# Transposes and gate products of a background chain recorded as one run on TensorE

## The chip, the cores and the metric

The kernel runs on one core of one Trainium2 chip. The metric is device time in microseconds (us) of one launch; lower is better. Engines are named as the profile names them: PE is TensorE (PEld its weight loads), DVE is VectorE, ACT is ScalarE, POOL is GpSimd, SP issues the DMAs of the weight stream. PSUM is the memory into which PE writes; SBUF is the working memory that the other engines read and write.

## What is computed

A decoder block for 256 tokens of width 2048, in float32. Cut to what matters:

```python
xn = rms_norm(x)
proj = xn @ w_in                       # 2048 x 26720, split in three
y_ssm = ssd_branch(p_ssm) @ w_branch_ssm   # 8 groups, causal conv, gated, scanned in chunks of 128
y_gdn = gdn_branch(p_gdn) @ w_branch_gdn   # 16 heads, causal conv, triangular inverse, gated
h = x + (gates[0] * y_ssm + gates[1] * y_gdn) @ w_out
hn = rms_norm(h)
q = hn @ w_q                           # 8 heads x 2 x 128
s = q . sub_keys                       # two lists of 128 scores per head, top 16 of each,
                                       # top 16 of the 256 sums: 128 experts of 16384 per token
out = rms_norm(h + sum over chosen experts of gate * gelu(u[e] . hn) * v[e])
```

The kernel does the last line densely: it multiplies hn with the whole table u (16384 x 2048), multiplies the activations with a gate that is zero for every expert that wasn't chosen, and multiplies the result with the whole table v.

## The kernel before

**The stream.** All large matrices (w_in, the two branch matrices, w_out, w_q, u, v) pass through one stream of 512 KB units of 128 x 1024 floats. SP loads a unit into one of four `raw` buffers. `Stream.split` (line 100) cuts it into a high part `whi` (ACT, line 107) and a low part `wlo` (DVE, line 108), which go into one of three cut buffers; `Stream.next` (line 113) hands a cut unit to PE and splits up to two units ahead. `product` (line 373) makes three products of each piece (lines 384 to 386: high by high, high by low, low by high) of 512 columns for both halves of the tokens: 12 products of 512 columns to a unit. PE takes its instructions strictly in order.

**Background chains.** Everything else is written as Python generators: `gdn_gen` and `ssm_gen` for the two mixers, `mt_gen` and `h_gen` for transposes of activations, `score_gen` for the keys, `gate_gen` for the dense gate, `act_gen` for the activations of each piece of u. After each piece of a unit, `product` calls `bg.step()`: it runs up to two chains that are due, each up to its next `yield`. Whether a chain is due is decided while the program is recorded, from a table of estimated durations (class `Clock`): a chain's next step is due once what it recorded last is estimated to be through. So a `yield` costs a chain at least a wait until its last result is through, and the position of each instruction in an engine's order is fixed when the program is built. `bg.drain(es)` runs chains until the named ones are finished, with no product of the stream in between.

**What a step holds.** A step that transposes takes one PSUM tile (`ps_tile()`, name `pst`, four buffers), records four transposes of 128x128 (`tr`, line 316) into it, records the evacuation on ACT or DVE, and yields; the next step does the other half. `score_gen` makes its scores (line 1056) in the same way.

**The dense gate.** `gate_gen` (line 1083) comes after the four score chains. For every four tokens, `build(n)` (line 1124) makes two one-hot tiles on DVE (`oa`, line 1130; `ob`, line 1131, a single buffer) and multiplies `ob` by the gates on POOL (`b2`, line 1132). Eight f16 products of 128x128 (line 1149) turn them into a PSUM tile, ACT copies that into `stages` (line 1151), and after each second build 512 KB are written to the DRAM tile `gdr` (line 1153). There are 64 builds; build n+2 is recorded in the step that multiplies build n.

**Where it is needed.** The table u is done in 32 pieces (`for u in range(32)`, line 1199), with one `act_gen` for each, which writes 512 KB to `hdr`. Before piece 31 the kernel drains `gate_gen`, then ACT issues two loads of 1 MB from `gdr` (`gate_load`, line 1184) and two of 512 KB from `hdr` (`coef_load`, line 1188). The first coefficients (`coef`, lines 1194 to 1197) are made at k == 13 of piece 31. Then comes the stage of table v (lines 1222 to 1228).

Of the kernel before, what the change touches and what calls it, by code (L numbers as in the profile page):

```python
# [240 lines left out]
def block(ctx, tc, nc, I, out, dbg=None):  # L241
# [488 lines left out]
    def ssm_gen(g, pt, bce, zg, yref):  # L730
# [25 lines left out]
        y = mx.tile([128, 2, 512], F, name="ys", bufs=1)  # L756
        for tb in range(2):
            p = ps_tile()
            for c in range(4):
                tr(p[:, c * 128:(c + 1) * 128], xT[:, c, tb * 128:(tb + 1) * 128])  # L760
            p3 = p.rearrange("p (h d) -> p h d", h=8)
# [53 lines left out]
        for c2 in range(2):  # L815
            p = ps_tile().rearrange("p (a b) -> p a b", a=2)
            for a in range(2):
                c = 2 * c2 + a
                for tb in range(2):
                    tr(p[:, a, tb * 128:(tb + 1) * 128], y[:, tb, c * 128:(c + 1) * 128])  # L820
            for a in range(2):
                c = 2 * c2 + a
                split_t(yh[:, c, :], yl[:, c, :], p[:, a, :], snw[:, 4 * g + c:4 * g + c + 1])
            yield
# [53 lines left out]
    def mt_gen(n):  # L878
        if n == 3:
            yield  # L880
        for k2 in (2 * n, 2 * n + 1):
            p = ps_tile().rearrange("p (a b) -> p a b", a=2)
            for a in range(2):
                for tb in range(2):
                    tr(p[:, a, tb * 128:(tb + 1) * 128], accs[0][:, tb, (2 * k2 + a) * 128:(2 * k2 + a + 1) * 128])
            split_t(mh[:, 2 * k2:2 * k2 + 2, :], ml[:, 2 * k2:2 * k2 + 2, :], p, 0.5)
            yield
# [107 lines left out]
    def h_gen(n):  # L995
        for c2 in range(2):
            p = ps_tile().rearrange("p (a b) -> p a b", a=2)
            for a in range(2):
                k = 4 * n + 2 * c2 + a
                for tb in range(2):  # L1000
                    tr(p[:, a, tb * 128:(tb + 1) * 128], h[:, tb, k * 128:(k + 1) * 128])
# [41 lines left out]
    def score_gen(i, q):  # L1043
        qT = pp.tile([128, 4, T], F, name="p4", bufs=6)
        for c2 in range(2):
            p = ps_tile().rearrange("p (a b) -> p a b", a=2)
            for a in range(2):
                for tb in range(2):
                    tr(p[:, a, tb * 128:(tb + 1) * 128], q[:, tb, (2 * c2 + a) * 128:(2 * c2 + a + 1) * 128])
            S.activation(qT[:, 2 * c2:2 * c2 + 2, :], p, AF.Copy)  # L1050
            yield
        sc = pp.tile([128, 2, 4, 128], F, name="p4", bufs=6)
        for tb in range(2):
            p = ps_tile().rearrange("p (a b) -> p a b", a=4)
            for a in range(4):
                PE.matmul(p[:, a, :], qT[:, a, tb * 128:(tb + 1) * 128], keys[:, 4 * i + a, :], start=True, stop=True)
# [26 lines left out]
    def gate_gen(score_es):  # L1083
# [53 lines left out]
        nxt = [build(0)]  # L1137
        yield
        nxt.append(build(1))
        for n in range(64):  # L1140
            yield
            oa, b2 = nxt.pop(0)
            if n < 62:
                nxt.append(build(n + 2))
            stage = stages[:, (n // 2) % 4]
            p = ps_tile().rearrange("p (a b) -> p a b", a=4)
# [214 lines left out]
```

## Time and profile before

| | |
|---|---|
| median of 3 runs | 3410.59 us (3410.57 to 3413.02) |
| the profiled execution's own time | 3411.41 us |
| span of the profiled execution | 3409.6 us |
| PE busy | 3374.3 us, 99% of the span |
| DVE, ACT, POOL busy | 2248.6, 1732.8, 533.6 us |
| mean granted clock of PE | 0.997 |
| piece 31 of u begins on PE | 2668.61 us |
| last gate product begins | about 2570.4 us |

A timeline row has the start in us, the duration in us, engine, line, operation, the tiles written and read, the shapes, the number of merged instructions, and in brackets the idle time of the engine just before with what ended it. A duration of PE holds the pipeline's fill, so the distance from one start to the next is what an instruction costs there. "ACTq" is ACT's queue issuing a DMA.

### The profile page before, as it was taken

How to read it: one execution, taken by the hardware profiler on the slowest of the kernel's cores; microseconds unless marked ns; L12 is line 12 of the kernel's file. 1: busy time of each engine (PE TensorE's matmuls, PEld its weight loads, DVE VectorE, ACT ScalarE, POOL GpSimd, SP SyncE). 2: the span in 40 equal slices, each digit the busy share in tenths (PEclk: the TensorE clock that was granted, in tenths of full speed). 3: DMA queues.
4: the chain of work that ended last, by engine and by line, in shares of the span. 5: the costliest groups of instructions: out<-in, count | busy, mean ns of one | idle time of the engine just before them, and what ended most of it. 6: DMA issues, size and time to landing. Idle time of an engine off the chain costs nothing.

```text
span 3409.6 us, 43675 instructions
## 1 busy us (share of the span) xinstructions
PE 3374.3 (99%) x15958; PEld 2773.3 (81%) x15958; DVE 2248.6 (66%) x3214; ACT 1732.8 (51%) x2308; POOL 533.6 (16%) x835
## 2 busy tenths in 40 slices
PE   9999999999999999999999999999999999999998
PEld 7888887878888888888788888888888788888886
DVE  6666776766677777777665888766664455555555
ACT  6555555554445454544444544556565444444444
POOL 0435253545001000000000000133320000000000
PEclk9999999999999999999999999999999999999999
DMA  7655564555555555555566566677776877777765
GB/s 263 194 162 172 162 187 152 181 161 179 180 187 182 183 182 185 185 174 193 186 218 186 172 212 213 212 232 233 234 232 219 266 242 242 243 237 242 243 231 161
DMA packets 254776, 692.33 MB, mean 203 GB/s; under 512 B 31248, under 2 KB 92000, under 8 KB 254304
## 3 DMA queue, kind: packets, MB, share of 16 engines
q1 hardware_dynamic: 164960, 594.03, 54.3%
q10 hardware_dynamic: 84000, 87.60, 7.8%
q0 software_dynamic: 5600, 7.91, 0.8%
q8 instruction: 125, 2.05, 0.2%
q14 instruction: 91, 0.75, 0.1%
HBM read 650.13 MB, written 39.41 MB: 202 GB/s over the span
## 4 chain that ended last, share of the span: by engine, by line
PE 95%; DVE 3%; ACT 1%; issue 1%; ACTq 0%; DMA 0%; POOL 0%; POOLq 0%; DVEq 0%; SPq 0%
PE acc L384 22%; PE acc L385 22%; PE acc L386 22%; PE acc L1223 3%; PE acc L1222 3%; PE acc L1228 3%; PE pst L1222 3%; PE pst L1223 3%; PE pst L1228 3%; PE pst L316 3%; DVE wlo L108 1%; PE pst L1149 1%; PE pst L781 1%; DVE t L459 1%; ACT whi L107 0%
## 5 line engine op out<-in xcount | busy, mean ns | idle before, releaser
L108 DVE TENSOR_TENSOR wlo<-raw,whi 128x1024 fp32r<-128x1024 f32 (+1 forms) x1129 | 1415.2, 1261 | 895.8 <-ACT whi L107 894.6
L107 ACT ACTIVATE whi<-raw 128x1024 fp32r<-128x1024 f32 (+1 forms) x1129 | 1184.0, 1053 | 945.3 <-PE acc L386 531.4
L384 PE MATMUL acc<-whi,t 128*128 128x512 f32 (+2 forms) x2848 | 1150.9, 404 | 8.7 <-ACT whi L107 8.7
L385 PE MATMUL acc<-wlo,t 128*128 128x512 f32 (+2 forms) x2848 | 1109.8, 390 | 6.2 <-DVE wlo L108 6.0
L386 PE MATMUL acc<-whi,t 128*128 128x512 f32 (+2 forms) x2848 | 1109.2, 389 | 0.0
L385 PEld LDWEIGHTS acc<-wlo,t 128*128 128x128 f32 x2848 | 537.5, 189 | 115.0 <-DVE wlo L108 12.3
L384 PEld LDWEIGHTS acc<-whi,t 128*128 128x128 f32 x2848 | 537.0, 189 | 113.5 <-ACT whi L107 8.9
L386 PEld LDWEIGHTS acc<-whi,t 128*128 128x128 f32 x2848 | 536.4, 188 | 113.7
L1132 POOL TENSOR_TENSOR b<-ob,gp 128x1024 f16<-128x1024 f16 x64 | 121.5, 1898 | 608.0 <-DVE ob L1131 608.0
L384 PE MATMUL acc<-whi,yh 128*128 128x512 f32 x512 | 207.8, 406 | 0.0
L385 PE MATMUL acc<-wlo,yh 128*128 128x512 f32 x512 | 200.1, 391 | 1.6 <-DVE wlo L108 1.6
L1223 PE MATMUL pst<-wlo,t 128*128 128x512 f32 x512 | 199.3, 389 | 2.1 <-DVE wlo L108 2.1
L386 PE MATMUL acc<-whi,yl 128*128 128x512 f32 x512 | 199.9, 390 | 0.0
L1222 PE MATMUL pst<-whi,t 128*128 128x512 f32 x512 | 199.4, 389 | 0.0
L1222 PE MATMUL acc<-whi,t 128*128 128x512 f32 x512 | 199.2, 389 | 0.0
L1223 PE MATMUL acc<-wlo,t 128*128 128x512 f32 x512 | 199.2, 389 | 0.0
L1228 PE MATMUL pst<-whi,t 128*128 128x512 f32 x508 | 156.4, 389 | 0.0
L1228 PE MATMUL acc<-whi,t 128*128 128x512 f32 x508 | 156.4, 389 | 0.0
L459 DVE SCALAR_TENSOR_TENSOR t<-pst,cols,t 128x255 f32<-128x255 f32 x336 | 135.8, 472 | 20.6 <-ACT t L455 20.5
L1151 ACT ACTIVATE t<-pst 128x512 f32<-128x512 f32 x64 | 76.8, 1199 | 80.9 <-PE pst L1149 80.9
L385 PEld LDWEIGHTS acc<-wlo,yh 128*128 128x128 f32 x512 | 96.3, 188 | 23.3 <-DVE wlo L108 2.9
L1223 PEld LDWEIGHTS pst<-wlo,t 128*128 128x128 f32 x512 | 96.1, 188 | 22.3 <-DVE wlo L108 2.4
(294 smaller groups left out, 3279.4 us busy)
## 6 DMA issues: line engine op xcount, KB each, us to landing
raw<-w_in SPq DMA_DIRECT2D x408, 512.0 KB
raw<-u SPq DMA_DIRECT2D x256, 512.0 KB
raw<-v SPq DMA_DIRECT2D x256, 512.0 KB
raw<-w_gdn SPq DMA_DIRECT2D x64, 512.0 KB
raw<-w_ssm SPq DMA_DIRECT2D x64, 512.0 KB
raw<-w_out SPq DMA_DIRECT2D x32, 512.0 KB
raw<-w_q SPq DMA_DIRECT2D x32, 512.0 KB
hdr<-ht ACTq DMA_DIRECT2D x32, 512.0 KB
```

The lines of the kernel that those rows point to most:

```text
L107: self.nc.scalar.activation(hi[:, s], t[:, s], AF.Copy)
L108: self.nc.vector.tensor_tensor(lo[:, s], t[:, s], hi[:, s].bitcast(F), op=OP.subtract)
L316: PE.transpose(dst, src, ident)
L384: PE.matmul(o, xa, h_, start=k == 0, stop=False)
L385: PE.matmul(o, xa, l_, start=False, stop=False)
L386: PE.matmul(o, xb, h_, start=False, stop=k == nk - 1)
L459: V.scalar_tensor_tensor(dst[:, s:], src[:, :T - s], w[:, c, k:k + 1], dst[:, s:], op0=OP.mult, op1=OP.add)
L1132: G.tensor_tensor(b2, ob[:, None, :, :].to_broadcast([128, 2, 4, 128]), gp[:, :, ts, None].to_broadcast([128, 2, 4, 128]), op=OP.mult)
L1151: S.activation(stage[:, :, q:q + 4].rearrange("p i t -> p t i"), p, AF.Copy, scale=1.0 / GSCALE)
L1222: PE.matmul(o_, a, hi[:, s], start=i2 == 0, stop=False)
L1223: PE.matmul(o_, a, lo[:, s], start=False, stop=False)
L1228: PE.matmul(acc[tb][2 * hv + n], b, hi[:, n * 512:(n + 1) * 512], start=False, stop=False)
```

## The change

At each of these places a chain now takes two PSUM tiles at once, records all its transposes (or products) into both in one go, and then evacuates the two tiles in two steps as before: `conv_silu`, `ssm_gen` (two places), `mt_gen`, `h_gen`, `score_gen` (two places), `gate_gen`, `act_gen`. In `conv_silu` the input tile is also released (`unread.pop(0)`) after the transposes. `gate_gen` is rewritten: four builds are made ahead, one to a step; then for each of 32 pairs of builds a step records 16 products into two tiles, both evacuations and the write to `gdr`, and the next two builds follow in steps of their own. `oa` and `b2` get four buffers instead of three; `ob` keeps one.

```diff
     def conv_silu(pool, src, nch, chunk_of, w, bias, dst):
         y = pool.tile([128, 4, T], F, name="t4", bufs=NT4[0])
+        ps = []
         for i0 in range(0, nch, 2):
             p = ps_tile().rearrange("p (a b) -> p a b", a=2)
             for a in range(2):
                 for tb in range(2):
                     tr(p[:, a, tb * 128:(tb + 1) * 128], src(tb, i0 + a))
+            ps.append(p)
+        unread.pop(0)
+        for i0, p in zip(range(0, nch, 2), ps):
             conv([(y[:, i0 + a, :], p[:, a, :], chunk_of(i0 + a)) for a in range(2)], w, bias)
             yield
-        unread.pop(0)
...
         def build(n):
             ts = slice(4 * n, 4 * n + 4)
-            oa = pp.tile([128, 4, 128], F16, name="oa", bufs=3)
+            oa = pp.tile([128, 4, 128], F16, name="oa", bufs=4)
             ob = pp.tile([128, 4, 128], F16, name="ob", bufs=1)
-            b2 = pp.tile([128, 2, 4, 128], F16, name="b2", bufs=3)
+            b2 = pp.tile([128, 2, 4, 128], F16, name="b2", bufs=4)
...
-        nxt = [build(0)]
-        yield
-        nxt.append(build(1))
-        for n in range(64):
+        nxt = []
+        for n in range(4):
+            nxt.append(build(n))
             yield
-            oa, b2 = nxt.pop(0)
-            if n < 62:
-                nxt.append(build(n + 2))
-            stage = stages[:, (n // 2) % 4]
-            p = ps_tile().rearrange("p (a b) -> p a b", a=4)
-            for t in range(4):
-                for s in range(2):
-                    PE.matmul(p[:, t, :], oa[:, t, :], b2[:, s, t, :], start=s == 0, stop=s == 1)
-            q = (n % 2) * 4
-            S.activation(stage[:, :, q:q + 4].rearrange("p i t -> p t i"), p, AF.Copy, scale=1.0 / GSCALE)
-            if n % 2:
-                S.dma_start(gdr[n // 2], stage)
+        for m in range(32):
+            stage = stages[:, m % 4]
+            pair = [nxt.pop(0), nxt.pop(0)]
+            ps = [ps_tile().rearrange("p (a b) -> p a b", a=4) for _ in range(2)]
+            for (oa, b2), p in zip(pair, ps):
+                for t in range(4):
+                    for s in range(2):
+                        PE.matmul(p[:, t, :], oa[:, t, :], b2[:, s, t, :], start=s == 0, stop=s == 1)
+            for q, p in enumerate(ps):
+                S.activation(stage[:, :, 4 * q:4 * q + 4].rearrange("p i t -> p t i"), p, AF.Copy, scale=1.0 / GSCALE)
+            S.dma_start(gdr[m], stage)
+            for n in (2 * m + 4, 2 * m + 5):
+                if n < 64:
+                    yield
+                    nxt.append(build(n))
+            yield
...
     def act_gen(u, ps):
...
-        for c2 in range(2):
-            p = ps_tile().rearrange("p (a b) -> p a b", a=2)
-            for a in range(2):
-                for tb in range(2):
-                    tr(p[:, a, tb * 128:(tb + 1) * 128], a_[:, tb, (2 * c2 + a) * 128:(2 * c2 + a + 1) * 128])
+        ps = [ps_tile().rearrange("p (a b) -> p a b", a=2) for _ in range(2)]
+        for a in range(4):
+            for tb in range(2):
+                tr(ps[a // 2][:, a % 2, tb * 128:(tb + 1) * 128], a_[:, tb, a * 128:(a + 1) * 128])
+        for c2, p in enumerate(ps):
             S.activation(ht[:, 2 * c2:2 * c2 + 2, :], p, AF.Copy)
             yield
```

The other places (`ssm_gen`, `mt_gen`, `h_gen`, `score_gen`) are written like `act_gen`. In the changed kernel the lines of the build are 1132 (`oa`), 1133 (`ob`) and 1134 (`b2`), the gate products 1150, their evacuation 1152, `gate_load` 1189, `coef_load` 1193, the Gelu of `act_gen` 1173 and its evacuation 1181.

**PE, one piece of table u (`act_gen`).** p is the activation tile, cst the identity. Before, the eight transposes stand as two fours around two pieces of a unit:

```order
L386 MATMUL acc<-whi,t_15362 128x512
L316 MATMUL pst<-cst,p_23268 128x128 x4
L384 MATMUL acc<-whi,t_15361 128x512
L385 MATMUL acc<-wlo,t_15361 128x512
L386 MATMUL acc<-whi,t_15362 128x512
L384 MATMUL acc<-whi,t_15361 128x512
L385 MATMUL acc<-wlo,t_15361 128x512
L386 MATMUL acc<-whi,t_15362 128x512
L316 MATMUL pst<-cst,p_23268 128x128 x4
L384 MATMUL acc<-whi,t_15361 128x512
```

After, at the same place in another piece:

```order
L385 MATMUL acc<-wlo,t_15361 128x512
L386 MATMUL acc<-whi,t_15362 128x512
L316 MATMUL pst<-cst,p_21970 128x128 x8
L384 MATMUL acc<-whi,t_15361 128x512
L385 MATMUL acc<-wlo,t_15361 128x512
```

The second four moved up behind the first. Over the whole program the runs of background work between two products of the stream go from 418 to 320; the gate products go from 64 runs of eight (16 of them with four transposes in the same run) to 24 runs of sixteen and one last run.

**DVE, the end of `gate_gen`.** Before, with the last two builds (oa and ob) between splits of units, and 44 splits after them until the first coefficient (L1194):

```order
L1130 TENSOR_TENSOR oa<-iob,i1T 128x512
L1131 TENSOR_TENSOR ob<-iob,i2T 128x512
L108 TENSOR_TENSOR wlo<-raw,whi 128x1024 x2
L1130 TENSOR_TENSOR oa<-iob,i1T 128x512
L1131 TENSOR_TENSOR ob<-iob,i2T 128x512
L108 TENSOR_TENSOR wlo<-raw,whi 128x1024 x44
L1194 TENSOR_TENSOR p_23440<-p_23440,m_23436 128x1024
L1197 TENSOR_TENSOR t_23435<-p_23440,t_23435 128x1024
```

After, from the splits of the first two units of piece 31 on:

```order
L108 TENSOR_TENSOR wlo_23144<-raw_23047,whi_23143 128x1024
L108 TENSOR_TENSOR wlo_23162<-raw_23066,whi_23161 128x1024
L1132 TENSOR_TENSOR oa_23184<-iob_16075,i1T_16077 128x512
L1133 TENSOR_TENSOR ob_23185<-iob_16075,i2T_16078 128x512
L1132 TENSOR_TENSOR oa_23203<-iob_16075,i1T_16077 128x512
L1133 TENSOR_TENSOR ob_23204<-iob_16075,i2T_16078 128x512
L1132 TENSOR_TENSOR oa_23230<-iob_16075,i1T_16077 128x512
L1133 TENSOR_TENSOR ob_23231<-iob_16075,i2T_16078 128x512
```

and the last two of these builds, up to the split of the third unit of piece 31:

```order
L1132 TENSOR_TENSOR oa_23395<-iob_16075,i1T_16077 128x512
L1133 TENSOR_TENSOR ob_23396<-iob_16075,i2T_16078 128x512
L1132 TENSOR_TENSOR oa_23401<-iob_16075,i1T_16077 128x512
L1133 TENSOR_TENSOR ob_23402<-iob_16075,i2T_16078 128x512
L108 TENSOR_TENSOR wlo_23460<-raw_23090,whi_23459 128x1024
```

The last 14 builds (50 to 63) have moved into the drain ahead of piece 31, with no split between them. On PE the products of builds 48 to 63 and the eight transposes of piece 30 stand there too, behind the last product of piece 30 and ahead of the first of piece 31.

**ACT, the same place.** Before:

```order
L107 ACTIVATE whi<-raw 128x1024 x6
L1168 ACTIVATE p_23431<-acc,r_16065 128x512 x2
L1184 DMA m_23436<-gdr 128x16x128 x2
L1188 DMA p_23440<-hdr 128x1024
L1188 DMA p_23442<-hdr 128x1024
L107 ACTIVATE whi<-raw 128x1024
```

After, from the last but one write of `gdr` on:

```order
L1153 DMA gdr<-t_19054 128x1024
L1152 ACTIVATE t_19054<-pst 128x4x128 x2
L1153 DMA gdr<-t_19054 128x1024
L1189 DMA m_23449<-gdr 128x16x128 x2
L1193 DMA p_23453<-hdr 128x1024
L1193 DMA p_23455<-hdr 128x1024
L107 ACTIVATE whi<-raw 128x1024 x7
```

The loads from `gdr` now stand directly behind the last write to it; the second of them reads what that write wrote and waits for it. The `whi` behind them is the third unit of piece 31.

## Rows read from the trace of the kernel before

**Rows 1.** The page: busy time of PE with its share of the span and instructions, and the granted clock of PE in 40 slices of the span, in tenths.

```profile
PE 3374.3 (99%) x15958; PEld 2773.3 (81%) x15958; DVE 2248.6 (66%) x3214; ACT 1732.8 (51%) x2308; POOL 533.6 (16%) x835
...
PEclk9999999999999999999999999999999999999999
```

**Rows 2.** What PE waited for over the whole span: us in total, times, longest.

```profile
PE acc L384 <- ACT whi L107: 8.7, 2, 6.3
PE acc L385 <- DVE wlo L108: 7.6, 14, 0.8
...
PE pst L655 <- ACT mm L651: 1.8, 2, 1.6
```

**Rows 3.** Timeline of PE around four runs of background work: eight gate products; eight gate products and four transposes; four transposes; eight transposes.

```profile
2570.18 0.40 PE L386 MATMUL acc<-whi,t 128*128 128x512 f32 x1
2570.42 0.62 PE L1149 MATMUL pst<-b,oa 128*128 128x128 f16 x8
...
2571.16 0.40 PE L385 MATMUL acc<-wlo,t 128*128 128x512 f32 x1
...
2555.40 0.39 PE L386 MATMUL acc<-whi,t 128*128 128x512 f32 x1
2555.63 0.62 PE L1149 MATMUL pst<-b,oa 128*128 128x128 f16 x8
2556.09 0.61 PE L316 MATMUL pst<-cst,p 128*128 128x128 f32 x4
...
2556.76 0.39 PE L385 MATMUL acc<-wlo,t 128*128 128x512 f32 x1
...
2602.94 0.39 PE L386 MATMUL acc<-whi,t 128*128 128x512 f32 x1
2603.17 0.60 PE L316 MATMUL pst<-cst,p 128*128 128x128 f32 x4
...
2603.84 0.39 PE L385 MATMUL acc<-wlo,t 128*128 128x512 f32 x1
...
1720.51 0.39 PE L386 MATMUL acc<-whi,t 128*128 128x512 f32 x1
1720.74 1.03 PE L316 MATMUL pst<-cst,t 128*128 128x128 f32 x8
...
1721.85 0.40 PE L385 MATMUL acc<-wlo,t 128*128 128x512 f32 x1
```

**Rows 4.** The line of the build on POOL over all its instructions: number, duration in ns (least, median, most), first and last start.

```profile
L1132 POOL TENSOR_TENSOR b<-ob,gp x64: 1896/1897/1900, 2172.7 to 2563.6; 128x1024 f16<-128x1024 f16 x64
```

**Rows 5.** Timeline of DVE and of POOL around the last build.

```profile
2562.19 0.68 DVE L1130 TENSOR_TENSOR oa<-iob,i1T 128x512 f16<-128x512 f16 x1
2562.79 0.69 DVE L1131 TENSOR_TENSOR ob<-iob,i2T 128x512 f16<-128x512 f16 x1
2564.58 2.03 DVE L108 TENSOR_TENSOR wlo<-raw,whi 128x1024 fp32r<-128x1024 f32 x1 [1.10 <-ACT whi L107]
...
2563.62 1.90 POOL L1132 TENSOR_TENSOR b<-ob,gp 128x1024 f16<-128x1024 f16 x1 [4.38 <-DVE ob L1131]
```

**Rows 6.** Timeline of POOL and of DVE where POOL's instruction came second (at 1277), and where it ran alone (at 1257).

```profile
1257.78 1.29 POOL L799 TENSOR_TENSOR ys<-ys,zg 128x512 f32<-128x512 f32 x1 [18.87 <-DVE ys L783]
1277.07 2.21 POOL L799 TENSOR_TENSOR ys<-ys,zg 128x512 f32<-128x512 f32 x1 [18.01 <-DVE ys L793]
...
1276.91 1.22 DVE L108 TENSOR_TENSOR wlo<-raw,whi 128x1024 fp32r<-128x1024 f32 x1
```

**Rows 7.** Timeline of POOL and of DVE at the end of the span, where DVE waits for a result of POOL.

```profile
3402.69 0.55 POOL L313 TENSOR_TENSOR r<-m,half 128x1 f32<-128x1 f32 x1 [3.65 <-DVE m L1242]
...
3403.28 1.28 DVE L1248 SCALAR_TENSOR_TENSOR t<-t,r,t 128x1024 f32<-128x1024 f32 x1 [0.67 <-POOL r L313]
```

**Rows 8.** Timeline of PE, DVE and ACT at the start of piece 31.

```profile
2668.61 0.39 PE L384 MATMUL acc<-whi,t 128*128 128x512 f32 x1
...
2671.33 0.60 PE L316 MATMUL pst<-cst,p 128*128 128x128 f32 x4
...
2677.53 0.79 PE L384 MATMUL acc<-whi,t 128*128 128x512 f32 x1 [2.39 <-ACT whi L107]
...
2667.18 1.23 DVE L108 TENSOR_TENSOR wlo<-raw,whi 128x1024 fp32r<-128x1024 f32 x1 [1.50 <-ACT whi L107]
...
2668.81 3.25 ACTq L1184 DMA_DIRECT2D m<-gdr  x2
2672.09 4.23 ACTq L1188 DMA_DIRECT2D p<-hdr  x2
2676.43 1.06 ACT L107 ACTIVATE whi<-raw 128x1024 fp32r<-128x1024 f32 x1 [6.93 <-DMA m<-gdr]
```

**Rows 9.** Timeline of ACT behind the last but one gate product, and the DMA queues from 2572.3 to 2576.1 us (packets, MB, share of 16 engines); q10 is ACT's.

```profile
2571.10 1.20 ACT L1151 ACTIVATE t<-pst 128x512 f32<-128x512 f32 x1
2572.32 0.33 ACTq L1153 DMA_DIRECT2D gdr<-t  x1
...
q10 hardware_dynamic: 144, 0.52, 49.8%
```

**Rows 10.** Two stretches at the start of piece 31: length, busy time and number of instructions on PE, PEld, DVE, ACT and POOL, granted clock of PE, share and rate of the DMA engines.

```profile
2677.50:2684.00 6.50, 6.00 (x13) 4.42 (x14) 3.67 (x3) 2.95 (x5) 0.00 (x0) 0.50 1.05 390
2684.00:2690.00 6.00, 6.00 (x28) 4.90 (x26) 2.45 (x2) 2.49 (x3) 0.00 (x0) 0.99 0.64 230
```

More of the change, by code (lines that the diff above doesn't have):

```diff
@@ L756, in ssm_gen @@
         y = mx.tile([128, 2, 512], F, name="ys", bufs=1)
+        ps = [ps_tile() for _ in range(2)]
         for tb in range(2):
-            p = ps_tile()
             for c in range(4):
-                tr(p[:, c * 128:(c + 1) * 128], xT[:, c, tb * 128:(tb + 1) * 128])
-            p3 = p.rearrange("p (h d) -> p h d", h=8)
+                tr(ps[tb][:, c * 128:(c + 1) * 128], xT[:, c, tb * 128:(tb + 1) * 128])
+        for tb in range(2):
+            p3 = ps[tb].rearrange("p (h d) -> p h d", h=8)
             V.tensor_tensor(xdt[:, tb], p3, dt[:, tb, 8 * g:8 * g + 8, None].to_broadcast([128, 8, 64]), op=OP.mult)
@@ L814, in ssm_gen @@
         yh, yl = yref
-        for c2 in range(2):
-            p = ps_tile().rearrange("p (a b) -> p a b", a=2)
-            for a in range(2):
-                c = 2 * c2 + a
-                for tb in range(2):
[L820 to L823, printed above, removed]
-            yield
+        ps = [ps_tile().rearrange("p (a b) -> p a b", a=2) for _ in range(2)]
+        for c in range(4):
+            for tb in range(2):
+                tr(ps[c // 2][:, c % 2, tb * 128:(tb + 1) * 128], y[:, tb, c * 128:(c + 1) * 128])
+        for c in range(4):
+            split_t(yh[:, c, :], yl[:, c, :], ps[c // 2][:, c % 2, :], snw[:, 4 * g + c:4 * g + c + 1])
+            if c % 2:
+                yield
     def z_gate(ps, lst, zg):
@@ L880, in mt_gen @@
             yield
[L881 to L885, printed above, removed]
+        ps = [ps_tile().rearrange("p (a b) -> p a b", a=2) for _ in range(2)]
+        for c in range(4):
+            for tb in range(2):
+                tr(ps[c // 2][:, c % 2, tb * 128:(tb + 1) * 128], accs[0][:, tb, (4 * n + c) * 128:(4 * n + c + 1) * 128])
+        for k2, p in zip((2 * n, 2 * n + 1), ps):
             split_t(mh[:, 2 * k2:2 * k2 + 2, :], ml[:, 2 * k2:2 * k2 + 2, :], p, 0.5)
@@ L995, in h_gen @@
     def h_gen(n):
[L996 to L1001, printed above, removed]
+        ps = [ps_tile().rearrange("p (a b) -> p a b", a=2) for _ in range(2)]
+        for a in range(4):
+            for tb in range(2):
+                tr(ps[a // 2][:, a % 2, tb * 128:(tb + 1) * 128], h[:, tb, (4 * n + a) * 128:(4 * n + a + 1) * 128])
+        for c2, p in enumerate(ps):
             for a in range(2):
@@ L1044, in score_gen @@
         qT = pp.tile([128, 4, T], F, name="p4", bufs=6)
[L1045 to L1049, printed above, removed]
+        ps = [ps_tile().rearrange("p (a b) -> p a b", a=2) for _ in range(2)]
+        for a in range(4):
+            for tb in range(2):
+                tr(ps[a // 2][:, a % 2, tb * 128:(tb + 1) * 128], q[:, tb, a * 128:(a + 1) * 128])
+        for c2, p in enumerate(ps):
             S.activation(qT[:, 2 * c2:2 * c2 + 2, :], p, AF.Copy)
@@ L1052, in score_gen @@
         sc = pp.tile([128, 2, 4, 128], F, name="p4", bufs=6)
+        ps = [ps_tile().rearrange("p (a b) -> p a b", a=4) for _ in range(2)]
         for tb in range(2):
[L1054 removed]
             for a in range(4):
[L1056 removed]
+                PE.matmul(ps[tb][:, a, :], qT[:, a, tb * 128:(tb + 1) * 128], keys[:, 4 * i + a, :], start=True, stop=True)
+        for tb, p in enumerate(ps):
             S.activation(sc[:, tb], p, AF.Copy)
@@ L1170, in act_gen @@
         yield
-        for c2 in range(2):
-            p = ps_tile().rearrange("p (a b) -> p a b", a=2)
-            for a in range(2):
-                for tb in range(2):
-                    tr(p[:, a, tb * 128:(tb + 1) * 128], a_[:, tb, (2 * c2 + a) * 128:(2 * c2 + a + 1) * 128])
+        ps = [ps_tile().rearrange("p (a b) -> p a b", a=2) for _ in range(2)]
+        for a in range(4):
+            for tb in range(2):
+                tr(ps[a // 2][:, a % 2, tb * 128:(tb + 1) * 128], a_[:, tb, a * 128:(a + 1) * 128])
+        for c2, p in enumerate(ps):
             S.activation(ht[:, 2 * c2:2 * c2 + 2, :], p, AF.Copy)
```

4 lines of the change are left out of this document (2 added, 2 removed).

## The prediction

> **What bounds the kernel now.** First I read the summary page of the profile. PE is busy 99% of the span, and no other engine over 66%; its granted clock is at full level in every slice [rows 1]. So whatever PE executes or waits for is paid in full, and work of the others costs only where PE waits for it. Second, the waits of PE: they are few, some 20 us in all, and the two longest are waits of a first product (line 384) for the high part on ACT [rows 2]. One of those two lies at the start of piece 31 of table u, where a gap of 2.39 us stands [rows 8]. There I looked third, because the order of the changed kernel differs most there: the chain of the dense gate, which before ended some 98 us ahead of piece 31 (last gate products about 2570.4, piece 31 from 2668.61 [rows 3, 8]), is now not finished when the drain comes.
>
> **Fewer runs on PE.** A run's price is the time from the product of the stream in front of it to the second one behind it, less two ordinary steps. An ordinary step is (2671.33 - 2668.61) / 12 = 0.227 us [rows 8]. Four transposes: 0.90 - 0.45 = 0.45; eight in one run: 1.34 - 0.45 = 0.89; so joining two fours saves under 0.01 us. Eight gate products: 0.98 - 0.45 = 0.53 by that row, 0.52 in the other runs alike; eight with four transposes behind them: 1.36 - 0.45 = 0.91, so eight more instructions in an existing run cost 0.91 - 0.45 = 0.46 [rows 3]. Sixteen gate products in one run are then about 0.52 + 0.46 = 0.98. The gate products cost 48 x 0.52 + 16 x 0.46 = 32.3 us before. After, 24 runs of sixteen stay in the stream, 23.5 us: 8.8 less, of which some 7.8 are not saved but moved into the drain. Some 64 joined pairs of transposes bring 0.4. Together 9.2 us leave the stream.
>
> **The drain ahead of piece 31.** The gate chain now has three steps to a pair of builds where it had two, so it runs out of pieces: 14 builds and the products of 16 are recorded in the drain, behind the last product of piece 30 and ahead of the first of piece 31. PE executes in order, so piece 31 can't start before the last gate product, and that needs the last `b2` from POOL. `b2` takes 1.90 us [rows 4]; before it ran beside the stream and cost nothing, and that cover is gone. The chain from build to build: `ob` has one buffer, so the next `ob` on DVE waits for `b2`, and the next `b2` waits for that `ob`. Steps: `ob` 0.69, 0.14 until POOL starts (2562.79 + 0.69 to 2563.62), `b2` 1.90 [rows 5], 0.04 from POOL's end to DVE's start (3402.69 + 0.55 to 3403.28) [rows 7]: 2.77 us if the next `oa` runs under `b2`.
>
> It probably doesn't. Two rows show that such instructions exclude each other. The split that started at 2564.58 under a `b2` took 2.03 instead of 1.23 us and ended 1.09 after `b2` [rows 5, 8]; and POOL's instruction that started 0.16 after a split took 2.21 instead of 1.29 and ended 1.15 after the split's end [rows 6]. The next `oa` follows `ob` on DVE at once (0.60 from start to start), so it stands ahead of `b2`, and `b2` can only end 1.90 - 0.14 = 1.76 after `oa`'s end. A build is then 0.60 + 0.68 + 1.76 + 0.04 = 3.08 us. The rows show this for splits in float32, not for `oa` in f16 with a repeated operand. The Trainium skill, page "SBUF — State Buffer", section "Who interferes with whom", says that a DVE instruction with two SBUF inputs contends with a GpSimd instruction that reads SBUF, and that the one that issues second fully blocks. By that rule `oa` is such an instruction whatever its type, and a build is 3.08 us; read as a matter of float32 alone it is 2.77, and the sum below 4.0 us smaller. I take 3.08, by the two rows.
>
> DVE is through with the last split ahead of the drain at 2667.18 + 1.23 = 2668.41 [rows 8], so on the old time axis: 0.60 for the first `oa`, 13 builds of 3.08, the last build without an `oa` behind it (0.69 + 0.14 + 1.90), 0.05 and eight products of 0.056 (0.45). The last gate product ends at 2668.41 + 0.60 + 40.04 + 2.73 + 0.50 = 2712.3, 43.7 us after piece 31 began before. The transposes of piece 30 and the products of the earlier builds fit into POOL's time; so do the evacuations on ACT (2 x 1.20 and 0.33 against 6.2 to a pair [rows 9]).
>
> **Behind the drain.** Two units of piece 31 are already split, so PE can run 5.4 us. The third unit's `whi` stands on ACT behind the last evacuation and the loads. Before, the third unit began at 2677.53, 8.9 us after piece 31 began, because ACT's queue was occupied with the four loads from 2668.81 to 2676.43, 7.6 us [rows 8]. Now ACT starts the last evacuation about 0.3 after the last products (2570.42 plus seven steps of 0.056 to 2571.10), needs 1.20, and 0.33 for the write [rows 3, 9]: the loads begin some 1.85 us after the last product. If they occupy ACT as long as before, and `whi` to PE takes 1.1 as before, the third unit begins 1.85 + 7.6 + 1.1 = 10.6 us after the last gate product. The new wait for the last write (issued 2572.32, its 0.52 MB through by 2576.1 [rows 9], so up to 3.8 us) may lie inside the 7.6, since the first load transfers meanwhile, or come on top: 10.6 to 13.6. If the loads no longer clog ACT's queue, it is 1.85 + 3.4 + 1.1 + 1.1, about 7.5. I take 10.6, nearest to the row. Queued behind the waiting ACT are the splits, DVE's low parts and PE.
>
> The third unit thus begins 43.7 + 10.6 - 8.9 = **45.4 us later** in its place, and the stream behind it is bound by PE, so nothing absorbs it.
>
> **The clock.** Behind the gap of 2.39 us PE's clock was at half, 1.2 GHz, for 6.5 us and then full again [rows 10]; that cost about 3.3 us. In the drain PE is nearly idle for 43 us, so it probably falls there; at half rate the first two units take 10.9 us, about what ACT needs anyway. I expect it to recover in these two units or once more behind the third, as before: 0, with 3.4 either way.
>
> **Elsewhere.** The order of the mixers' steps shifts too. PE's other waits come to about 12 us, the longest 1.6 [rows 2]; I take no change there, within 4 us: a second PSUM tile that waits for its evacuation can make a step late.
>
> **The sum.** 45.4 - 9.2 = +36.2 us: span 3409.6 to 3445.8, the profiled execution 3411.41 to 3447.6, and on the median of the runs, which lies 0.8 below that execution, 3410.59 to **3446.8 us**, 1.06% slower.
>
> **Rivals.**
> 1. `oa` runs under `b2`: 13 x 0.31 = 4.0 less, 3442.8. For it: no row shows `oa` there. Against: rows 5 and 6. A drain of about 39.5 instead of 43.7 us would tell.
> 2. The wait for the last write comes on top of the clogged loads, and the clock stays at half behind the third unit: 3.0 + 3.4 more, 3453.2. For it: the second load can't be issued before the write has landed. Against: the first is under way meanwhile.
> 3. The mixers gain stalls of the kind of line 655 (1.6 us [rows 2]), some followed by a half clock: five of them would be 8 us or more, 3455 and up.
> 4. On the other side: a switch between the stream and a background run costs PE more than the four runs above show, so that 98 fewer runs pay for the drain. It decides from 45.4 / 98 = 0.46 us a run. A whole run of four transposes costs 0.45, and eight in one run cost twice four to 0.01; so it stands on nothing but the four rows being untypical. At 0.55 a run the time would be 3402. If the drain cost nothing at all (the chain hidden after all), only the joining would be left: 64 gate runs made 32, 32.3 - 32 x 0.98 + 0.4 = 1.3 us, 3409.3, which is no change.
>
> **How the numbers follow.** The forecast with its own bounds has 0.74, rival 1 has 0.10, rival 2 has 0.07, rival 3 has 0.05, not slower has 0.04 (faster 0.02, the same 0.02). Below, the range takes in rival 1, the short wait on ACT (3.1) and part of the clock: 3437. Above, rival 2 and part of the mixers' 4 us: 3457. Over 0.2% (6.8 us, about what a measurement of this kernel can tell from no change): slower 0.96, same 0.02, faster 0.02.
>
> **What would show it.** In the profile of the changed kernel: a stretch of 40 to 45 us ahead of piece 31 in which PE does 128 gate products and waits for `b2` on POOL; starts of `b2` 3.1 us apart there (2.8 under rival 1); ACT's `whi` behind the loads 8 to 12 us late; a half clock around it; runs of eight transposes near 0.89 and of sixteen gate products near 0.98. It would be wrong if `b2` came faster than every 2 us, if the products of piece 31 stood among the gate products, or if the time before 2600 us differed by more than 10 us.

## The result, and the profile after

The changed kernel takes 3450.28 us (median of 4 runs, 3449.59 to 3451.88), beside 3411.44 us for the kernel before (4 runs, 3410.57 to 3413.02): 1.0116 times as long, 95% interval 1.0104 to 1.0128. Its profiled execution took 3451.88 us, with a span of 3450.1 us, 40.5 more than before.

The page of the changed kernel: PE's busy time and its clock by slices, to be held against [rows 1].

```profile
PE 3378.1 (98%) x15958; PEld 2787.4 (81%) x15958; DVE 2274.3 (66%) x3214; ACT 1725.8 (50%) x2308; POOL 560.3 (16%) x835
...
PEclk9999999999999999999999999999999799999999
```

PE has the same 15958 instructions and is hardly longer busy (3.8 us). The time went into waiting, and one slice of 40 shows a lower clock. What PE waited for, to be held against [rows 2] (us in total, times, longest):

```profile
PE pst L1150 <- POOL b L1134: 28.1, 14, 2.5
PE acc L384 <- ACT whi L107: 11.2, 2, 6.8
PE acc L385 <- DVE wlo L108: 9.9, 14, 2.3
PE pst L316 <- POOL o L708: 2.5, 1, 2.5
PE pst L316 <- ACT kt L597: 2.3, 3, 0.9
```

The first row is new: 14 waits of gate products for POOL's `b2`, one for each build in the drain. The third has the same count as before, but 2.3 us more and a longest of 2.3 instead of 0.8; the last two are new too. Those belong to the mixers, at the start of the program.

The drain on POOL's timeline, first three and last builds, answers to [rows 4]:

```profile
2664.57 2.21 POOL L1134 TENSOR_TENSOR b<-ob,gp 128x1024 f16<-128x1024 f16 x1 [8.93 <-DVE ob L1133]
2667.66 2.21 POOL L1134 TENSOR_TENSOR b<-ob,gp 128x1024 f16<-128x1024 f16 x1 [0.87 <-DVE ob L1133]
2670.74 2.21 POOL L1134 TENSOR_TENSOR b<-ob,gp 128x1024 f16<-128x1024 f16 x1 [0.87 <-DVE ob L1133]
...
2704.64 1.90 POOL L1134 TENSOR_TENSOR b<-ob,gp 128x1024 f16<-128x1024 f16 x1 [0.87 <-DVE ob L1133]
```

Thirteen cycles lie between the first and the last start: (2704.64 - 2664.57) / 13 = 3.08 us. Each takes 2.21 us but the last, which takes 1.90 like the builds before: it alone has no `oa` behind it. DVE at the same place answers to [rows 5]:

```profile
2662.01 1.22 DVE L108 TENSOR_TENSOR wlo<-raw,whi 128x1024 fp32r<-128x1024 f32 x1
2663.14 0.69 DVE L1132 TENSOR_TENSOR oa<-iob,i1T 128x512 f16<-128x512 f16 x1
2663.74 0.68 DVE L1133 TENSOR_TENSOR ob<-iob,i2T 128x512 f16<-128x512 f16 x1
2664.34 0.69 DVE L1132 TENSOR_TENSOR oa<-iob,i1T 128x512 f16<-128x512 f16 x1
2666.82 0.69 DVE L1133 TENSOR_TENSOR ob<-iob,i2T 128x512 f16<-128x512 f16 x1 [1.79 <-POOL b L1134]
```

`oa` runs from 2664.34 to 2665.03, and the `b2` that started at 2664.57 ends at 2666.78: 1.75 us after `oa`, when 1.76 had been forecast for a `b2` that does no work under `oa`. Then `ob` follows 0.04 us after `b2`.

PE around the drain, first and last rows of it, and the third unit of piece 31, to be held against [rows 8]:

```profile
2662.69 0.39 PE L386 MATMUL acc<-whi,t 128*128 128x512 f32 x1
...
2664.68 1.06 PE L1150 MATMUL pst<-b,oa 128*128 128x128 f16 x16
2666.84 0.61 PE L1150 MATMUL pst<-b,oa 128*128 128x128 f16 x8 [1.11 <-POOL b L1134]
...
2706.58 1.01 PE L1150 MATMUL pst<-b,oa 128*128 128x128 f16 x8 [1.75 <-POOL b L1134]
2707.35 0.78 PE L384 MATMUL acc<-whi,t 128*128 128x512 f32 x1
...
2718.77 0.80 PE L384 MATMUL acc<-whi,t 128*128 128x512 f32 x1 [4.49 <-ACT whi L107]
```

Piece 30's last product starts at 2662.69; one step later, at 2662.92, piece 31 would have begun. It begins at 2707.35: 44.4 us. Its third unit begins 11.42 us after that (before: 8.92). ACT in this stretch shows why:

```profile
2707.63 1.11 ACT L1152 ACTIVATE t<-pst 128x512 f32<-128x512 f32 x1 [1.68 <-PE pst L1150]
2708.78 0.33 ACTq L1153 DMA_DIRECT2D gdr<-t  x1
2709.13 3.56 ACTq L1189 DMA_DIRECT2D m<-gdr  x2
2712.72 4.90 ACTq L1193 DMA_DIRECT2D p<-hdr  x2
2717.66 2.95 ACT L107 ACTIVATE whi<-raw 128x1024 fp32r<-128x1024 f32 x3 [8.92 <-issue]
```

The four loads hold ACT from 2709.13 to 2717.66, 8.53 us (before 7.6), and only then comes the `whi` for which PE waits. The stretches of the drain and behind it answer to [rows 10] (length; busy time on PE, PEld, DVE, ACT, POOL; PE's clock; DMA share and GB/s):

```profile
2662.90:2707.30 44.40, 15.84 (x137) 13.26 (x137) 18.35 (x29) 18.18 (x19) 30.65 (x14) 0.57 0.30 119
2707.30:2714.00 6.70, 6.70 (x27) 5.37 (x25) 0.00 (x0) 1.11 (x1) 0.00 (x0) 0.80 0.71 196
...
2718.80:2724.00 5.20, 4.74 (x11) 3.42 (x12) 3.45 (x3) 1.82 (x2) 0.00 (x0) 0.54 0.96 341
2724.00:2730.00 6.00, 6.00 (x28) 4.92 (x28) 2.45 (x2) 2.17 (x3) 0.00 (x0) 1.00 0.60 216
```

In the drain PE is busy for 15.84 of 44.4 us and POOL is the busiest engine. The clock falls to its lower level in it, is back in the first two units of piece 31, and is low once more behind the third, as before.

A run of sixteen gate products in the stream, to be held against [rows 3]:

```profile
2499.97 0.39 PE L386 MATMUL acc<-whi,t 128*128 128x512 f32 x1
2500.20 1.07 PE L1150 MATMUL pst<-b,oa 128*128 128x128 f16 x16
2501.07 0.48 PE L384 MATMUL acc<-whi,t 128*128 128x512 f32 x1
2501.39 0.40 PE L385 MATMUL acc<-wlo,t 128*128 128x512 f32 x1
...
2503.70 0.39 PE L386 MATMUL acc<-whi,t 128*128 128x512 f32 x1
...
2505.97 0.39 PE L384 MATMUL acc<-whi,t 128*128 128x512 f32 x1
```

Its price is 2501.39 - 2499.97 - 0.45 = 0.97, which is also the mean of the 24 runs; eight transposes cost 0.88 on average. Both are as forecast. But from 2501.39 on ten steps take 2.31 us, and the next ten, from 2503.70, take 2.27. More of that below.

**Where the time went.** The stream has the same products in the same order in both kernels, so the k-th product of one trace can be set beside the k-th of the other. After minus before, by their starts:

| place | later by |
|---|---|
| product 1200 of the stream | +10.0 us |
| product 4800 | +8.1 |
| product 8400, before the gate | +5.9 |
| last product of piece 30 | -5.7 |
| first product of piece 31 | +38.8 |
| third unit of piece 31 | +41.2 |
| ninth unit of piece 31, and still product 12000 | +40.4 |

So the mixers lost 8.1 us, the stream behind them gained 13.8 (8.1 + 5.7), and the drain with what follows it cost 44.4 + 2.5 - 0.8. What the fewer runs save ahead of product 4800 lies inside the 8.1.

### The profile page after: what moved, and what is told of

Read it like the earlier page. It is cut to its first block, busy times and chain, and to the rows that moved or that the text cites. A ratio compares the mean times of both kernels' runs of the same rounds, so it can differ in the third digit from the quotient of the medians.

```text
span 3450.1 us, 43697 instructions
## 1 busy us (share of the span) xinstructions
PE 3378.1 (98%) x15958; PEld 2787.4 (81%) x15958; DVE 2274.3 (66%) x3214; ACT 1725.8 (50%) x2308; POOL 560.3 (16%) x835
## 4 chain that ended last, share of the span: by engine, by line
PE 93%; DVE 3%; ACT 2%; POOL 1%; issue 1%; DMA 0%; ACTq 0%; POOLq 0%; SPq 0%; DVEq 0%
PE acc L384 22%; PE acc L385 22%; PE acc L386 22%; PE acc L1228 3%; PE acc L1227 3%; PE acc L1233 3%; PE pst L1228 3%; PE pst L1227 3%; PE pst L1233 3%; PE pst L316 3%; POOL b L1134 1%; DVE wlo L108 1%; PE pst L785 1%; PE pst L1150 1%; DVE t L459 1%
## 5 line engine op out<-in xcount | busy, mean ns | idle before, releaser
L108 DVE TENSOR_TENSOR wlo<-raw,whi 128x1024 fp32r<-128x1024 f32 (+1 forms) x1129 | 1444.3, 1290 | 887.8 <-ACT whi L107 885.8
L384 PE MATMUL acc<-whi,t 128*128 128x512 f32 (+2 forms) x2848 | 1139.5, 400 | 11.2 <-ACT whi L107 11.2
L384 PEld LDWEIGHTS acc<-whi,t 128*128 128x128 f32 x2848 | 537.0, 189 | 118.8 <-ACT whi L107 11.7
L1134 POOL TENSOR_TENSOR b<-ob,gp 128x1024 f16<-128x1024 f16 x64 | 132.3, 2068 | 731.2 <-DVE ob L1133 731.2
L537 POOL TENSOR_TENSOR ct<-cu,cy 16x15 f32<-16x15 f32 (+7 forms) x240 | 112.7, 469 | 41.8 <-DMA cu<-am 25.4
```

The lines of the kernel that those rows point to most:

```text
L108: self.nc.vector.tensor_tensor(lo[:, s], t[:, s], hi[:, s].bitcast(F), op=OP.subtract)
L384: PE.matmul(o, xa, h_, start=k == 0, stop=False)
L537: G.tensor_tensor(tm[:, :k, :n], u[:, :k, k:k + 1].to_broadcast([16, k, n]), y[:, k:k + 1, k:].to_broadcast([16, k, n]), op=OP.mult)
L1134: G.tensor_tensor(b2, ob[:, None, :, :].to_broadcast([128, 2, 4, 128]), gp[:, :, ts, None].to_broadcast([128, 2, 4, 128]), op=OP.mult)
```

## The experiments

All were run in five rounds with the kernel before on the same chip: e1 to e4 beside 3411.36 us (21 runs), e5 to e8 beside 3410.20 (28), e11 and e12 beside 3411.67 (15).

### The drain: the steps of the gate chain

**e1_gate_old**: the changed kernel with the `build` and loop of the old `gate_gen`; all other joins stay.

```diff
-        for m in range(32):
-            pair = [nxt.pop(0), nxt.pop(0)]
...
+        for n in range(64):
+            yield
+            oa, b2 = nxt.pop(0)
+            if n < 62:
+                nxt.append(build(n + 2))
...
```

Expected: 

> The changed kernel with the dense gate written as before (one build and eight products to a step). If the drain ahead of piece 31 is the cause, the gate is done some 98 us ahead of piece 31 again, the third unit of piece 31 begins about 9 us after its first, and what is left is the mixers' part (+8 us in the changed kernel's trace up to 1300 us) less the joined transposes (-3 to -4): 3415 to 3418 us. If the loss were spread over all the joined places, most of it stays: 3435 us or more.

Measured: 3412.51 us, ratio 1.0006 (0.9996 to 1.0015). No drain stands ahead of piece 31, and its third unit comes 8.42 us after its first product. The mixers' part is still there: +7.7 us at product 4800 of the trace. The time lies 2.5 us under the expectation. The joined transposes are not the reason: they gain 3.2 us, as expected (+7.7 at product 4800, +4.5 at the end of piece 30). Behind that the trace falls to +3.0: its third unit comes 0.5 us sooner, and the half clock behind it lasts 3.4 us instead of 6.8. And the profiled execution (3414.41) is the second longest of eleven, 1.9 above the median.

**e2_gate_only**: the kernel before with the new `gate_gen` alone (the diff above, the other way round).

Expected: 

> The kernel before with only the dense gate rewritten as in the change. By the drain theory the whole loss is here: piece 31 about 46 us late, 40 us of it in the drain with builds 3.08 us apart, less about 11 us of gate products that leave the stream: 3445 to 3448 us. If the other joined places carry the loss: 3430 us or less.

Measured: 3445.05 us, ratio 1.0103 (1.0087 to 1.0118). One function makes the drain and most of the slowdown, 33.7 of 38.8 us: `b2` starts every 3.08 us in a drain ahead of piece 31, and the clock is low there for 41.0 us and again for 6.8. With e1 this shows that the drain belongs to `gate_gen`, and that it doesn't need the other joins.

**e4_two_steps**: the changed kernel, runs of sixteen kept, but with the first of the two next builds recorded in the step that multiplies, so two steps to a pair as before.

```diff
             for n in (2 * m + 4, 2 * m + 5):
                 if n < 64:
-                    yield
                     nxt.append(build(n))
-            yield
+                    yield
+            if m > 29:
+                yield
```

Expected: 

> The changed kernel with two steps to a pair of builds instead of three: the first build of the next pair is recorded in the step that multiplies, all sixteen products still in one run. By the order the last gate products then stand 186 products of the stream ahead of piece 31. If the third step is what brought the drain, there is none, PE's clock falls only behind the third unit of piece 31 as before, and the time is that of the kernel with the old gate less 2 to 3 us (32 runs of 0.97 us for 64 of 0.5, and half as many slow tails): 3412 to 3416 us. If joining the products as such costs, 3420 us or more.

Measured: 3409.92 us, ratio 0.9998 (0.9989 to 1.0007). The last gate products now stand 186 products of the stream ahead of piece 31, there is no wait for POOL's `b2`, and 40 us are gone although each run still has sixteen products. The time is below the range expected; against e1 as measured it is 2.6 us shorter, the 2 to 3 that the expectation took. The length of the runs was not the cause; the third step of a pair was.

### The price of a build in the drain

**e3_ob2**: a second buffer for `ob` in the changed kernel.

```diff
-            ob = pp.tile([128, 4, 128], F16, name="ob", bufs=1)
+            ob = pp.tile([128, 4, 128], F16, name="ob", bufs=2)
```

Expected: 

> The changed kernel with two buffers for ob. If DVE's two one-hot instructions and POOL's product exclude each other, the starts of b2 in the drain stay 2.9 to 3.1 us apart (0.6 + 0.6 + 1.76) and the time within 2 us of the changed kernel's 3450. If only the single ob buffer made the chain, POOL runs through at 1.9 to 2.0 us a build and the drain is about 15 us shorter: 3435 us.

Measured: 3447.13 us, ratio 1.0109 (1.0094 to 1.0124), 3.2 us under the changed kernel where at most 2 had been expected, and far from 3435. Two builds on POOL's and on DVE's timeline in that kernel:

```profile
2670.02 2.21 POOL L1134 TENSOR_TENSOR b<-ob,gp 128x1024 f16<-128x1024 f16 x1 [0.69 <-DVE ob L1133]
2672.92 2.21 POOL L1134 TENSOR_TENSOR b<-ob,gp 128x1024 f16<-128x1024 f16 x1 [0.69 <-DVE ob L1133]
```

```profile
2669.80 0.68 DVE L1132 TENSOR_TENSOR oa<-iob,i1T 128x512 f16<-128x512 f16 x1
2670.40 2.38 DVE L1133 TENSOR_TENSOR ob<-iob,i2T 128x512 f16<-128x512 f16 x1
2672.70 0.68 DVE L1132 TENSOR_TENSOR oa<-iob,i1T 128x512 f16<-128x512 f16 x1
```

With two buffers nothing in the program keeps `ob` from running under `b2`, and it is issued there, at 2670.40. But it takes 2.38 us instead of 0.69 and ends 0.55 after `b2` (2672.78 against 2672.23): it was held until `b2` was through. Builds come every 2.90 us instead of 3.08. So the single buffer costs 0.18 us a build, 2.3 us over 13 of them; the rest of the cycle is the two engines shutting each other out. The Trainium skill, page "SBUF — State Buffer", section "Who interferes with whom", says that DVE and GpSimd share one pair of ports and that it is an exclusive lock; the rows agree, for f16 operands too.

### Behind the drain: the loads on ACT's queue

**e5_loads_early**: the kernel before, with the two loads of `gdr` (and the drain of the gate chain, which is through by then) moved from piece 31 to piece 30; the loads of `hdr` stay.

```diff
     for u in range(32):
+        if u == 30:
+            bg.drain([ge])
+            gg = [pp.tile([128, 32, 16, 8], F, name="m16", bufs=2) for _ in range(2)]
+            gate_load(0, 0)
+            gate_load(0, 1)
         if u == 31:
-            bg.drain([ge])
...
-            gate_load(0, 0)
-            gate_load(0, 1)
```

Expected: 

> The kernel before with only the two loads of 1 MB from gdr issued one piece earlier, ahead of piece 30; the two from hdr stay ahead of piece 31. If ACT's queue, filled by the four loads at once, is what holds the third unit of piece 31 (8.9 us after the first), the third unit comes after some 6.4 us (two units and eight transposes), no half clock follows it, and the time falls by 5 to 6 us: 3405 to 3407 us. If the loads only carry the wait with them, piece 30 has it instead: 3411 us.

Measured: 3405.24 us, ratio 0.9983 (0.9974 to 0.9992). ACT's two load issues in that kernel, and the 24 us around the start of piece 31 (columns as above):

```profile
2644.00 3.17 ACTq L1184 DMA_DIRECT2D m<-gdr  x2
...
2666.70 0.82 ACTq L1188 DMA_DIRECT2D p<-hdr  x2
```

```profile
2666.00:2690.00 24.00, 24.00 (x111) 19.86 (x111) 11.46 (x11) 12.43 (x15) 0.27 (x1) 1.00 0.74 252
```

The loads of `hdr` take 0.82 us to issue instead of 4.23 [rows 8], the third unit comes 6.39 us after the first product instead of 8.92, PE is busy without a gap, and the half clock is gone. So the wait ahead of the third unit comes from four load issues in a row on the engine that also makes `whi`, as the prediction had it, and it was there before the change.

### The mixers: joined transposes in conv_silu

**e7_conv_only**: the kernel before with the joined `conv_silu` alone.

```diff
+        ps = []
         for i0 in range(0, nch, 2):
             p = ps_tile().rearrange("p (a b) -> p a b", a=2)
...
+            ps.append(p)
+        unread.pop(0)
+        for i0, p in zip(range(0, nch, 2), ps):
             conv([(y[:, i0 + a, :], p[:, a, :], chunk_of(i0 + a)) for a in range(2)], w, bias)
             yield
-        unread.pop(0)
```

Expected: 

> The kernel before with only conv_silu joined as in the change (and its input tile released earlier). If the later mixers' stalls of the changed kernel (11.7 us of PE idle between 20 and 700 us against 4.4 before, in two of the four profiles followed by half clocks) come from here, they are here too: +7 us, up to 3.4 more with half clocks, less 1 us for 18 fewer runs: 3416 to 3420 us. If they come from the other joined places of the mixers, the idle time before 700 us stays near 4.4 us and the time at 3410 to 3412.

Measured: 3415.13 us, ratio 1.0013 (1.0004 to 1.0022), 4.9 us over the kernel before and 0.9 under the range expected; no half clock stands in the mixers of this trace. PE's waits over the span of that kernel have the new rows of the changed kernel again:

```profile
PE acc L385 <- DVE wlo L108: 9.5, 14, 2.3
...
PE pst L316 <- POOL o L708: 2.5, 1, 2.5
PE pst L316 <- ACT kt L597: 2.3, 3, 0.9
...
PE pst L607 <- ACT mm L636: 1.2, 1, 1.2
```

Between 20 and 700 us PE's idle time is 680 - 668.26 = 11.7 us, against 680 - 675.51 = 4.5 in the kernel before and 680 - 668.04 = 12.0 in the changed one. The joined `conv_silu` alone brings the mixers' stalls. Only the last two rows of these are, by their names, waits for the evacuation of a PSUM tile: `kt` and `mm` are what ACT reads out of one, and neither is an input of the instruction that waits. They come to 3.5 us; the others wait for a low part of the stream or for a result that isn't there yet.

**e6_conv_old**: e4 with the old `conv_silu` (the diff above, the other way round).

Expected: 

> The two-step kernel (gate without a drain) with conv_silu as before. If conv_silu makes the mixers' stalls, PE's idle time before 700 us goes back from 11.5 to 4 to 5 us: 3403 to 3406 us. If not, 3410 us as the two-step kernel.

Measured: 3405.28 us, ratio 0.9983 (0.9974 to 0.9992). PE's idle time from 20 to 700 us is back at 680 - 675.46 = 4.5 us. Against their own runs of the kernel before, e4 gained 1.4 us and this kernel 4.9, so the old `conv_silu` is worth 3.5 us here; in the two traces this kernel is 4.0 us ahead of e4 at product 4800 (+0.9 against +4.9). That is most of e7's loss of 4.9, from the other side.

**e11_conv_one_step**: e7 with both evacuations in the step of the transposes, so that no PSUM tile is held over a step.

```diff
         for i0, p in zip(range(0, nch, 2), ps):
             conv([(y[:, i0 + a, :], p[:, a, :], chunk_of(i0 + a)) for a in range(2)], w, bias)
-            yield
+        yield
```

Expected: 

> The kernel before with conv_silu joined, but with both evacuations recorded in the step of the transposes, so that no PSUM tile is held over a step. If the stalls of the joined conv_silu are PSUM tiles that come free late (2.3 us of waits of the transposes for the evacuation of a key tile in its trace), PE's idle time between 20 and 745 us falls from 12.5 us by 2 to 3 us, and more if the later ones follow from them: 3411 to 3413 us. If it is that the chains come to stand differently, the stalls lie elsewhere but sum up to as much or more (twelve operations of DVE in one step): 3415 us or more.

Measured: 3449.99 us, ratio 1.0116 (1.0100 to 1.0131), on the side of the second expectation, but ten times as far off as that had in mind. The waits of PE over its span:

```profile
PE acc L385 <- DVE wlo L108: 30.9, 24, 2.9
PE acc L384 <- ACT whi L107: 11.1, 3, 7.1
PE acc L386 <- DVE yl L332: 3.8, 2, 2.7
PE pst L316 <- ACT kt L597: 1.4, 2, 0.8
```

The stream's low parts come late 24 times, for 30.9 us: most of them stand on DVE directly behind the twelve instructions of a chain's convolution, 4.7 us of work in one step. Six half clocks between 889 and 1510 us add to it, and by product 6000 of the stream the kernel is 39.4 us behind. So the two-step evacuation, which the change kept, is what makes a joined `conv_silu` bearable.

For the cause of e7's stalls the run decides nothing. In the window that the expectation names, 20 to 745 us, PE's idle time falls from 725 - 712.40 = 12.6 to 725 - 714.68 = 10.3 us, by the 2 to 3 of the first theory, and the waits for `kt` there from 2.3 to 0.6. But e7's longest waits, 2.3 us for a low part and 2.5 for `o`, are gone as well, and others of up to 2.7 stand in their place: the edit moved every wait of that stretch, and not only those for a tile. The other theory, that the joining moves every later step of the mixers against the stream, fits too and wasn't isolated either.

### The stream: what a run costs beyond itself

**e12_rest**: the kernel before with the joins of `ssm_gen`, `mt_gen`, `h_gen`, `score_gen` and `act_gen` alone (edits as in the diff of the change): 364 runs of background work instead of 418, neither the gate nor `conv_silu` touched.

Expected: 

> The kernel before with the joins of ssm_gen, mt_gen, h_gen, score_gen and act_gen alone (gate and conv_silu as before). 54 fewer runs on PE. By the price of the four runs read before (joining two fours saves under 0.01 us) the time is that of the kernel before less 0.4 us. If each run also makes the ten products behind it slower, by 0.04 to 0.05 us together, as the steps of both traces say, it is 2 to 3 us faster, and the sum of the stream's steps over 226.67 ns falls from 13.2 to about 11 us.

Measured: 3408.56 us, ratio 0.9989 (0.9980 to 0.9998), 3.1 us by the medians. The span of the trace is 2.7 us shorter, but 0.9 of that comes behind the third unit of piece 31, where the half clock lasts 3.4 us instead of 6.8, and the trace starts 0.6 us late. From product 600 to the end of piece 30 it gains 2.4 us (+0.6 to -1.8). In each trace I took all steps of the stream that follow no wait and no run directly, and added up what each is longer than an ordinary step of 226.7 ns: 13.2 us before, 11.2 in e12, 8.7 in the changed kernel. The runs number 418, 364 and 320. So 98 runs fewer go with 4.5 us less of this, 0.046 us a run, and 54 runs fewer with 2.0, 0.037 a run. With the 0.4 us that the runs themselves save, the 2.0 make up e12's gain.

The three parts of the change by themselves (e2 +33.7, e7 +4.9, e12 -3.1 us) add up to 35.5 of its 38.8; the rest is within their intervals, that of e2 alone being 5 us to either side.

### The best of the parts

**e8_all**: e4's steps, the old `conv_silu`, e5's early loads, all other joins.

Expected: 

> All three: two steps to a pair, conv_silu as before, the gdr loads one piece earlier. The parts should add: 3410 - 5 - 6 = 3399 us, within 3; if the parts share one cause (one half clock, say), 3403 or more.

Measured: 3398.99 us, ratio 0.9967 (0.9955 to 0.9980), 11.2 us under the kernel before, and faster than both kernels. The parts add up: e6 gained 4.9 and e5 5.0 beside the same kernel before.

## Why the prediction was right, and what it missed

The forecast was 3446.8 us and the result 3450.28; sign, cause and place were right, and two terms of the sum were off in opposite directions. That the sum came within 3.5 us is in part luck, since those two errors (-4.6 and +8.1) half cancel. Term by term, by the trace:

| term, as the prediction named it | forecast | measured |
|---|---|---|
| fewer runs on PE | -9.2 | -13.8 |
| the drain ahead of piece 31 | +43.7 | +44.4 |
| the third unit behind it (10.6 - 8.9) | +1.7 | +2.5 (11.4 - 8.9) |
| the clock | 0 | -0.8 |
| elsewhere (the mixers) | 0 | +8.1 |
| sum, on the span | +36.2 | +40.4 |

The profiled execution of the changed kernel is the longest of its four; by the medians the difference is 3450.28 - 3411.44 = 38.8.

**The drain: right in every step.** It is 14 builds of 3.08 us behind a first `oa`, and e2 and e4 show that the third step of a pair makes it. The 0.7 us more: DVE's first `oa` started 0.2 us after piece 30's last step (2663.14 against 2662.92), where by [rows 8] 0.2 us before it had been taken; and the last eight products, at the lower clock, needed 0.8 instead of 0.5 us.

**Rival 1 is out.** `oa` doesn't run under `b2`; e3 shows the same exclusion with the engines' order reversed, DVE waiting for POOL.

**Behind the drain: right, 0.8 us too small.** The term "if they occupy ACT as long as before" was mis-sized: 8.53 us instead of 7.6. The wait for the last write thus lies mostly inside, as taken; rival 2's 3 us on top didn't come. Nor are the 0.9 us the price of that wait: in e2, with the same drain, the loads hold ACT for 7.1 us, and in e1 and e4, without a drain, for 7.1 and 7.0. The start (1.78 us after the last product, forecast 1.85) and the end (1.11, forecast 1.1) fit.

**The clock: right.** The low clock of the drain lasts into the first two units (41.0 us from 2669.0), which ACT's loads hide, and the one behind the third unit is as long as before, 6.8 us. The -0.8 is its start: 2.1 us ahead of that unit (2716.7 against 2718.77) instead of 0.2, so that more of it passes while PE waits.

**Fewer runs on PE: mis-sized, 4.5 us too little.** The prices of the runs themselves were right to 0.02 us. What was missing is behind them: some ten steps of the stream after a run take 227 to 233 ns on average instead of 226.7. The prediction's price ended with the second product behind a run and took all later steps as ordinary. e12 shows the gain by itself (2.4 us up to piece 31, where the prices without it give 0.4). Why the steps are longer is open.

**Elsewhere: mis-sized, +8.1 where 0 within 4 had been taken.** The prediction named the mechanism ("a second PSUM tile that waits for its evacuation can make a step late") and rival 3 its sign, but the price was put at nothing because the other waits of before came to "about 12 us, the longest 1.6". (The whole list, of which [rows 2] leaves out some lines, has 14.3 us beside those for `whi`, with a longest of 2.1 in the stage of table v; in the mixers 1.6 is right.) PE's idle time before 700 us grew by 7.5 us (12.0 against 4.5), with single waits of up to 2.5, and two half clocks of 3.4 us stand there instead of one. These are chance in part: e3 and e4 have the same waits in the mixers and no half clock there, and are 4.8 and 4.9 us late at product 4800 instead of 8.1. e7 and e6 put it on `conv_silu`. The mechanism named can be 3.5 us of the new waits by their names (e7), and e11 doesn't decide how much of them it is. What moves the stalls is open: the joining changes when each later step of the mixers is due, so that the order of all engines shifts there, and no run held the one and varied the other. That `conv_silu` now releases its input tile earlier can't be the cause: with a late release the program comes out the same, instruction by instruction.

**A sign that came true.** Of the signs of being wrong that the prediction named, two stayed out: `b2` came every 3.08 us, and no product of piece 31 stands among the gate products. The third came: the time before 2600 us differed by more than 10 us, +14.2 at product 2909 of the stream (799 us before; +8.0 at product 2400 and +8.2 at 3600) and -10.6 at product 10008 (2584 us), where part of it is gate products that moved into the drain. It points at the two terms that were mis-sized, the mixers and the fewer runs, and not at the drain.

**Not slower** failed on its price: it asked for 0.46 us more a run, and a run costs 0.04 beyond what was counted.

## What to carry to other kernels

Where a background chain advances by steps, count its steps against the work that is left until its drain: one `yield` more to a pair of builds cost 40 us here, and each run fewer saved 0.04 to 0.12 us (e12: 2.4 us for 54 runs; e1 to e4: 2.6 for 21). A chain that goes from DVE to POOL and back is hidden while it has slack; once it is on the path, each build costs about the sum of both engines' times, not the longer of them (3.08 us here, where POOL alone needs 1.90). Issue loads that share a queue with an engine on the path a piece before they are needed, and keep the evacuations of a joined run in separate steps.

## What the runs showed of the hardware

- After each run of background products some ten steps of the stream are on average up to 6 ns longer than ordinary ones, together about 0.04 us (2.31 us for ten steps, then 2.27). It stands in every trace that was summed; why it is so, none shows.
- An instruction shut out by the other engine isn't shown as waiting but as longer: `b2` 2.21 us instead of 1.90 behind `oa`, `ob` 2.38 instead of 0.69 behind `b2`.
- The same stall is followed by a half clock in one execution and not in another. Waits of 2.3 us at 251 and of 2.5 us at 659 in the mixers: a half clock of 3.4 us stands at both in the changed kernel and e1, none in e3, e4 and e7. In the mixers and behind the third unit of piece 31 it lasts 3.4 or 6.8 us where it comes.
- A DMA issue can hold its engine for microseconds: the two loads of `hdr` took 4.90 (changed kernel) and 4.23 us (before) to issue directly behind the loads of `gdr`, and 0.82 where the loads of `gdr` were long through (e5).
